# A list scheduler that counts weight transfers at 405 GB/s, and a last expert pair without fillers

## The chip, the cores and the metric

The kernel runs on one NeuronCore of one Trainium2 chip. The metric is the time of one execution on the device in microseconds; the time of the kernel before is the median of three runs. Four compute engines matter here: TensorE (PE, matmuls), VectorE (DVE), ScalarE (ACT) and GpSimd (POOL). SyncE (SP) issues every transfer between memory and the on-chip buffers, and 16 DMA engines carry them out.

## The reference, cut to what matters

A trunk of two layers over 272 tokens (16 meta tokens and 256) of width 1024. Each layer has a mixer and then a mixture of 16 experts; all inputs are float32.

```python
for layer in range(DEPTH):                       # 2
    if layer % 2 == 0:
        h = h + ssd_lru_mixer(rms_norm(h, ...), ...)          # "mixer0"
    else:
        h = h + multiscale_pool_mixer(rms_norm(h, ...), ...)  # "mixer1"
    h = h + hierarchical_moe(rms_norm(h, ffn_norm[layer]), ...)
return rms_norm(h[:, N_META:], norm_final)

def hierarchical_moe(hn, ...):                   # top-1 group, top-2 experts in it
    for e in range(MOE_EXPERTS):                 # 16
        hid = silu(tok @ w_gate[e]) * (tok @ w_up[e])        # 1024 x 512 each
        out = out + gates[:, e:e + 1] * (hid @ w_down[e])    # 512 x 1024
```

The weights of the experts are most of what is moved: 16 experts x 3 matrices x 2 MB in each of two layers, 201 MB of the 234 MB of the whole execution.

## The kernel before, in words

**Tiling.** The tokens of an expert are gathered into 64 slots. The experts are worked off in 8 pairs a layer (`p` = 0 to 7), each expert of a pair on its half of the output partitions. A pair takes 12 weight pieces of 1 MB, each a tile in one of 17 slots of the pool `hs`: 4 gate pieces, 4 up pieces, 4 down pieces. Gate and up pieces hold rows of 512 float32 (2 KB) and down pieces rows of 1024 (4 KB); the down pieces of each layer's last pair are cut by columns instead (256 or 128 float32 in a row), as are all pieces of `w_in` and `w_out` (256).

**What a pair does** (in `moe`): `gate_up` multiplies the gathered tokens by the gate pieces (PSUM tile `gb`, 4 quarters), then by the up pieces (`ub`), and DVE makes the hidden rows `sg`. `combine` adds the output of the pair before to the residual (`cmb`). Behind an odd pair `gather` collects the tokens of the next two pairs (`xgp`). `down` transposes `sg` on PE (`htp`), ACT copies that to `ht`, and PE multiplies by the down pieces (`yb`). `ptrans` (`ppt`, `pgs`) is small work for the next pair. A runtime branch (`overflow`, line 1576) sits behind the sixth pair's products as a barrier.

**What sets the order.** Nothing runs while the source is written: each call is recorded as an `Op` with a duration from `Program.cost`, and `Program.order`, a list scheduler, then fixes each engine's instruction order. It keeps a clock for each engine and one (`pipe`) for the transfers, which follow one another without overlap, each as long as its bytes over 358 GB/s. An operation may start when what it reads has been produced or has landed, by these clocks. Among the operations of an engine that can start within 60 ns of the earliest, the one first in the source goes first. On the chip the order of an engine is fixed; only the waits are real.

**Fillers.** Where the scheduler's clock leaves PE idle, `order` puts transposes of the identity into PE's stream (`wm`, line 735 in the trace), one for each 215, 200, 115, 110 or 100 ns of the gap, by the phase that `mark` has set. They compute nothing that is used. Within the pairs (`moe0p0` to `moe1p7`) there are none, with one exception: the phase `moe1p7`, which is all of the last pair of layer 1.

```python
if e == "PE" and self.filler and (op.phase[-2] != "p" or op.phase == "moe1p7"):
    gap = s - FILL0 - clock[e] if clock[e] else s - 650
    ...
    if op.phase == "moe1p7":
        gap, each = gap + FILL0 - FILL3, 110     # FILL3 = 200
    for _ in range(int(gap / each)):
        out.append(self.filler)
```

The fillers cost nothing on the scheduler's own clock: an operation behind them starts there when it would have started without them.

Of the kernel before, what the change touches and what calls it, by code (L numbers as in the profile page):

```python
# [55 lines left out]
class Program:  # L56
# [67 lines left out]
    def cost(self, key, method, out, reads, k):  # L124
        n = self.cols(out)
        ps_ = any(self.in_psum(r) for r in reads) or self.in_psum(out)
        m = max([n] + [self.cols(r) for r in reads])
        scal = sum(isinstance(k.get(w), bass.AP) for w in ("scale", "bias", "scalar", "scalar1"))
        scal += sum(self.cols(r) == 1 for r in reads if n > 1) if not scal else 0
        if method == "dma_start":  # L130
            dims = [tuple(d) for d in (reads[0] if out.tensor.name in self.bufs else out).ap]
            row = dims[-1][1] if dims[-1][0] == 1 else 1
            total = 1
            for _, q in dims:
                total *= q
            return max(total * 4, total // row * 160) / 358.0
        if key == "PE":
            passes, per = (1, 1 if n >= 256 else 4) if reads[0].dtype == F32R else (2, 2)
            if method == "transpose":
                passes, per = 1, 2  # L140
            share = {64: 2, 32: 4, 16: 4}.get(out.ap[0][1], 1)
            return passes * max(n * per / 2.4 / share, self.cols(reads[0]) / 1.2) + 2
        if key == "A":
            return (51 if ps_ else 94) + m / 1.2 + 93 * (scal + (k.get("accum_out") is not None))
        if method == "memset":
            return 35 + 0.84 * m if key == "G" else 7 + 1.04 * m
        if key == "V":
            if method == "reciprocal":
                return 69 + 6.25 * m
            if method in ("tensor_scalar", "tensor_copy"):  # L150
                return 66 + (1.04 if ps_ else 0.52) * m + 61 * scal
            return 68 + 1.042 * m + 61 * scal
        if method in ("affine_select", "iota"):
            return 170 + 0.57 * m
        return 176 + m * 3.33 if method in ("tensor_scalar", "tensor_copy") else 148 + 2.1 * m
# [225 lines left out]
def kernel(  # L381
# [19 lines left out]
    def ps(name):  # L401
        return prog.tile(psp, [128, 512], F32, "ps", 7, name)

    def one(name, shape, dt=F32):
        return prog.tile(const, shape, dt, name, 1, name)
# [4 lines left out]
    def b2(name):  # L410
        return prog.tile(bp, [128, 512], F32, "b2", 4, name)
# [4 lines left out]
    def mark(name):  # L416
        prog.phase = name
# [13 lines left out]
    def hs_free(n=1):  # L431
        live[0] -= n
# [126 lines left out]
    def pump(reserve=None, most=99):  # L559
        reserve = RES[0] if reserve is None else reserve  # L560
        while wpos[0] < len(wq) and live[0] < NHS - reserve and most > 0:
            most -= 1
            key, fn = wq[wpos[0]]
            pieces[key] = fn()
            wpos[0] += 1
# [871 lines left out]
    def moe(l):  # L1437
# [12 lines left out]
        def build_S(Q):  # L1450
            S = fr(b4("S")[:, : nt * 256]).rearrange("p (i s) -> p i s", i=nt)
            for i in range(nt):
                V.tensor_tensor(S[:, i, :].rearrange("p (e r) -> p e r", e=4),
                                rm[:, i, 4 * Q:4 * Q + 4, None].to_broadcast([128, 4, CAP]),
                                iota64[:, None, :].to_broadcast([128, 4, CAP]), op=ALU.is_equal)
            S_t[Q] = S
# [10 lines left out]
        def gather(Q):  # L1467
            gather_cols(S_t[Q], 256)
# [3 lines left out]
        def gu_quarter(kind, bank, p, q):  # L1472
            c0 = (p % 2) * 128
            ws = pieces[(kind, l, p, q)]
            for k in range(2):
                xk = xgh[q // 2][:, (2 * q + k) % 4, c0:c0 + 128]
                if isinstance(ws[0], list):
                    for c in range(4):
                        for e in range(2):
                            PE.matmul(bank[64 * e:64 * e + 64, c * 128:(c + 1) * 128], xk[:, 64 * e:64 * e + 64],  # L1480
                                      ws[e][k][c], start=False, stop=(k == 1 and c == 3))
                    continue
                for e in range(2):
                    PE.matmul(bank[64 * e:64 * e + 64, :], xk[:, 64 * e:64 * e + 64], ws[e][:, k, :],
                              start=(q == 0 and k == 0), stop=(q == 3 and k == 1))
            if p or q < 3:
                hs_free()
                pump()

        def gate_up(p, gs, gb, ub):  # L1490
            if p:
                for q in range(4):
                    gu_quarter("g", gb, p, q)
            sg = b2("sg")
            A.activation(sg, gb, AF.Silu, scale=gs[:, 1:2])
            if p:
                ub = ps("ub")
                for q in range(4):
                    gu_quarter("u", ub, p, q)
            V.scalar_tensor_tensor(sg, ub, gs[:, 1:2], sg, op0=ALU.mult, op1=ALU.mult)  # L1500
            return sg

        def ptrans(S, g3):

            pp = ps("ppt")
            for i, (o, sz) in enumerate(tl):
                PE.matmul(pp[:, o - off:o - off + sz], S[:, i, :], identr[:, :sz], start=True, stop=True)
            Pt = fr(b1("Pt"))
            A.copy(Pt[:, :NT], pp[:, :NT])
            pg = ps("pgs")  # L1510
            for i, (o, sz) in enumerate(tl):
                PE.matmul(pg[:, 0:3], ff(S[:, i, :]), g3[:, i, :], start=(i == 0), stop=(i == nt - 1))
            gs = prog.tile(bp, [128, 2], F32, "gs", 3, "gs")
            V.tensor_copy(gs[0:64], pg[0:64, 0:3:2])
            V.tensor_copy(gs[64:128], pg[64:128, 1:3])
            return Pt, gs
# [103 lines left out]
        def combine(yh, yl, Pt, c0=0, n=D):  # L1620
            if l == 0:
                for k in range(c0 // 128, (c0 + n) // 128):
                    c = ps("cmb")
                    PE.matmul(c[:, :T], yh[:, k * 128:(k + 1) * 128], Pt, start=True, stop=False)
                    PE.matmul(c[:, :T], yl[:, k * 128:(k + 1) * 128], Pt, start=False, stop=True)
                    V.tensor_tensor(hT[:, k, :], c[:, :T], hT[:, k, :], op=ALU.add)
            else:
                m = min(n, 512)
                for c1 in range(c0, c0 + n, m):
                    for i in range(2):  # L1630
                        c = ps("cmb")[:, 0:m]
                        PE.matmul(c, Pt[:, i * 128:(i + 1) * 128], yh[:, c1:c1 + m], start=True, stop=False)
                        PE.matmul(c, Pt[:, i * 128:(i + 1) * 128], yl[:, c1:c1 + m], start=False, stop=True)
                        V.tensor_tensor(tok[i][:, c1:c1 + m], c, tok[i][:, c1:c1 + m], op=ALU.add)
# [13 lines left out]
        for p in range(8):  # L1648
            mark(f"moe{l}p{p}")
            if (l, p) == (0, 7):  # L1650
                pools()
            if p % 2 == 0 and p < 6:
                build_S(p // 2 + 1)
            if p:
                Pt, gs = ptrans(S_t[p // 2][:, :, (p % 2) * 128:(p % 2) * 128 + 128], gate[:, :, p, :])
                gb = ps("gb")
            sg = gate_up(p, gs, gb, ub)
            if p == 7:
                A.activation(one("sqrt%d" % (l + 1), [128, 1]), sg[:, 0:1], AF.Sqrt, scale=0.0, bias=eps_t)
            if pend:  # L1660
                combine(*pend.pop())
            if p % 2 and p < 7:
                if p == 5:
                    prog.barrier(overflow)
                gather(p // 2 + 1)
                if p == 5:
                    hs_free(2)
                    RES[0] = RES0 if l == 0 else 0
                    pump()
            y = down(p, sg, gs, Pt)  # L1670
            if p < 7:
                pend.append((*y, Pt))
# [166 lines left out]
    slab_end(b1("end"), 16 - len(ends))  # L1839
    assert len(ends) == 16  # L1840
    moe(0)
    dump("h1", hT)
    pump()
# [3 lines left out]
    RES[0] = 0  # L1847
    pump()
    moe(1)
    final()  # L1850
    with tc.manual_schedule():
# [30 lines left out]
```

## Time and profile before

| | us |
|---|---|
| median of 3 runs | 753.37 |
| range of the runs | 751.78 to 756.37 |
| time of the profiled execution | 755.84 |
| span in its trace | 754.2 |
| PE busy | 714.1 |
| DVE, ACT, POOL busy | 313.9, 245.3, 150.4 |

The execution has five stretches: mixer0 to about 240 us, the experts of layer 0 to about 476, mixer1 to about 506, the experts of layer 1 to about 746, and the final norm. Times in the rows below are from the start of the span. Nearly all instructions were recorded through one helper, so they stand under line 102, and the name of the tile written tells them apart.

### The profile page before, as it was taken

Reading aid. Unit: us, or ns where it says so; the run is one execution under the profiler, and the core shown is the slowest. Engines: PE = TensorE matmul, PEld = TensorE weight load, DVE = VectorE, ACT = ScalarE, POOL = GpSimd, SP = SyncE. Lnnn points to the kernel's source line nnn. Section 1 sums busy time; section 2 is a strip of 40 time slices with the busy share of each in tenths; the row PEclk is TensorE's granted clock in tenths of the full one; section 3 lists DMA queues with packets and bytes.
Section 4 is the critical chain, followed back from the end, with each engine's and each line's share of the span. In section 5 each row is a group of like instructions: output and inputs, shape, how many; then the busy total and the mean of one; then the engine's idle time right before and its main releaser. Section 6 shows DMA issues by size and latency. Waiting matters only on the chain. (4 is left out here: it accounts for less than half of the span.)

```text
span 754.2 us, 11128 instructions
## 1 busy us (share of the span) xinstructions
PE 714.1 (95%) x4370; PEld 449.0 (60%) x4370; DVE 313.9 (42%) x701; ACT 245.3 (33%) x466; POOL 150.4 (20%) x149
## 2 busy tenths in 40 slices
PE   7999999997999999999998989989999999989995
PEld 5989889997899536436434433774354433353353
DVE  6779798779955012203221231571021211202204
ACT  4565476774353312113012012543130120121114
POOL 5654675466940000000000030000000000000003
PEclk7999999999999999999999999999999999999998
DMA  8993121937657879999999999988799999999951
GB/s 257 261 349 106 29 91 45 313 113 279 213 201 255 315 297 409 409 409 408 410 409 407 400 403 376 409 351 320 292 409 409 409 408 409 409 407 409 397 155 56
DMA packets 99622, 234.06 MB, mean 310 GB/s; under 512 B 12700, under 2 KB 51800, under 8 KB 99560
## 3 DMA queue, kind: packets, MB, share of 16 engines
q1 hardware_dynamic: 97448, 232.72, 82.2%
q8 instruction: 37, 0.61, 0.3%
q10 hardware_dynamic: 2112, 0.52, 0.3%
q14 instruction: 25, 0.20, 0.1%
HBM read 232.18 MB, written 1.05 MB: 309 GB/s over the span
## 5 line engine op out<-in xcount | busy, mean ns | idle before, releaser
L102 PE MATMUL yb<-w,ht 128*64 128x512 f32 (+2 forms) x592 | 116.4, 544 | 4.5 <-ACT ht L102 4.4
L102 PE MATMUL gb<-w,xg 128*64 128x512 f32 x496 | 115.7, 599 | 0.0
L102 PE MATMUL ub<-w,xg 128*64 128x512 f32 (+1 forms) x514 | 114.3, 583 | 0.1
L102 PE MATMUL pj<-Xh,wh 128*128 128x272 f32 x288 | 86.1, 301 | 1.3 <-DVE xT L102 1.3
L102 PE MATMUL pj<-Xl,wh 128*128 128x272 f32 x288 | 84.9, 295 | 0.0
L102 PE MATMUL pj<-Xh,wl 128*128 128x272 f32 x288 | 84.5, 294 | 0.0
L102 PEld LDWEIGHTS yb<-w,ht 128*64 128x64 f32 x592 | 40.7, 138 | 69.0 <-issue 56.1
L102 DVE SCALAR_TENSOR_TENSOR yl<-yb,gs,yh 128x512 fp32r<-128x512 f32 (+2 forms) x37 | 25.1, 677 | 129.5 <-ACT yh L102 120.3
L102 PEld LDWEIGHTS ub<-w,xg 128*64 128x64 f32 x514 | 36.8, 137 | 67.1 <-issue 65.2
L102 DVE SCALAR_TENSOR_TENSOR sg<-ub,gs,sg 128x512 f32<-128x512 f32 x16 | 12.0, 751 | 147.9 <-PE ub L102 146.6
L102 DVE TENSOR_TENSOR wl<-w,wh 128x1024 fp32r<-128x1024 f32 (+1 forms) x50 | 60.0, 1208 | 16.4 <-PE pj L102 8.8
L102 PEld LDWEIGHTS gb<-w,xg 128*64 128x64 f32 x496 | 32.7, 136 | 56.6 <-issue 49.7
L102 POOL TENSOR_TENSOR fo<-hT,gfin 128x256 f32<-128x256 f32 (+1 forms) x10 | 6.0, 627 | 292.6 <-DVE hT L102 292.4
L102 ACT ACTIVATE xg<-xgp,gain_e 128x256 f32<-128x256 f32 x64 | 30.2, 475 | 88.6 <-PE xgp L102 79.4
L102 POOL TENSOR_SCALAR wh<-w 128x512 fp32r<-128x512 f32 x25 | 52.2, 2087 | 30.6 <-PE pj L102 22.7
L102 PEld LDWEIGHTS pj<-Xh,wh 128*128 128x128 f32 x288 | 55.7, 194 | 2.8 <-DVE xT L102 1.5
L102 DVE TENSOR_TENSOR hT<-cmb,hT 128x272 f32<-128x272 f32 (+3 forms) x102 | 45.1, 495 | 28.1 <-PE cmb L102 28.0
L102 PEld LDWEIGHTS pj<-Xl,wh 128*128 128x128 f32 x288 | 55.8, 194 | 0.2
L102 ACT ACTIVATE yh<-yb,gs 128x512 fp32r<-128x512 f32 (+2 forms) x37 | 23.3, 630 | 99.6 <-PE yb L102 99.6
L102 PEld LDWEIGHTS pj<-Xh,wl 128*128 128x128 f32 x288 | 55.6, 193 | 0.0
L102 ACT CAST wh<-w 128x512 fp32r<-128x512 f32 (+1 forms) x51 | 42.0, 829 | 31.4 <-PE pj L102 18.6
L102 POOL TENSOR_TENSOR wl<-w,wh 128x512 fp32r<-128x512 f32 x29 | 43.5, 1502 | 41.2 <-issue 19.1
(348 smaller groups left out, 1035.4 us busy)
## 6 DMA issues: line engine op xcount, KB each, us to landing
w<-in_expert_w_down_dram SPq DMA_DIRECT2D x63, 1024.0 KB, 16.4
w<-in_expert_w_gate_dram SPq DMA_DIRECT2D x62, 1024.0 KB, 18.1
w<-in_expert_w_up_dram SPq DMA_DIRECT2D x62, 1024.0 KB, 15.3
w<-in_w_in_dram SPq DMA_DIRECT2D x17, 1024.0 KB, 9.6
w<-in_w_out_dram SPq DMA_DIRECT2D x8, 1024.0 KB, 11.4
ew<-in_expert_w_gate_dram SPq DMA_DIRECT2D x4, 512.0 KB
xs<-in_x_dram SPq DMA_DIRECT2D x2, 512.0 KB
w<-in_w_in_dram SPq DMA_DIRECT2D x2, 512.0 KB
```

The source lines that it names most:

```text
L102: return prog.add(key, lambda: call(*a, **k), reads, writes, prog.cost(key, method, out, reads, k), func)
```

## The change

It has two parts. The scheduler's cost of a transfer divides by 405 instead of 358 where the contiguous row has 512 or more elements (2 KB): that holds for the expert pieces other than the last pairs' down pieces, for the input tokens and the final gain, not for `w_in`, `w_out`, the pooling weights or the small parameters. And the phase is called `moe0pg` or `moe1pg` while `gate_up` of the last pair is recorded, so that the condition for fillers does not hold there; afterwards it is `moe0p7` or `moe1p7` again (for the other pairs the second `mark` sets the name that is already set). No operation that computes is added or removed, and no byte more or less is moved.

```diff
@@ Program.cost, method == "dma_start"
-            return max(total * 4, total // row * 160) / 358.0
+            return max(total * 4, total // row * 160) / (405.0 if row >= 512 else 358.0)
@@ moe, loop over the pairs
             if p:
                 Pt, gs = ptrans(S_t[p // 2][:, :, (p % 2) * 128:(p % 2) * 128 + 128], gate[:, :, p, :])
                 gb = ps("gb")
+            if p == 7:
+                mark(f"moe{l}pg")
             sg = gate_up(p, gs, gb, ub)
+            mark(f"moe{l}p{p}")
```

## Rows read from the trace of the kernel before

**Rows 1.** The page, busy time, share of the span and instructions of PE.
```profile
PE 714.1 (95%) x4370; PEld 449.0 (60%) x4370; DVE 313.9 (42%) x701; ACT 245.3 (33%) x466; POOL 150.4 (20%) x149
```

**Rows 2.** What PE waited for from 245 to 745 us: total us, times, longest.
```profile
PE xgp L102 <- PEq L1576: 4.8, 2, 2.5
PE htp L102 <- DVE sg L102: 4.7, 5, 1.0
PE yb L102 <- ACT ht L102: 4.4, 8, 0.7
```

**Rows 3.** Stretches: length, each engine's busy time (instructions), granted clock, DMA share, GB/s.
```profile
280.00:480.00 200.00, 192.60 (x1033) 92.14 (x1030) 50.74 (x133) 37.25 (x71) 6.41 (x28) 0.99 1.03 404
545.00:700.00 155.00, 147.08 (x706) 63.32 (x702) 29.87 (x56) 26.85 (x51) 0.00 (x0) 0.99 1.02 409
```

**Rows 4.** The same view, layer 1, pairs 1 to 7, first down product to first.
```profile
529.85:556.82 26.97, 26.86 (x143) 13.03 (x139) 5.38 (x10) 6.45 (x13) 0.00 (x0) 1.00 0.91 346
556.82:580.88 24.06, 23.90 (x114) 9.53 (x114) 4.87 (x10) 2.91 (x6) 0.00 (x0) 1.00 1.03 409
580.88:613.56 32.68, 30.76 (x147) 13.00 (x147) 5.96 (x14) 6.94 (x14) 0.00 (x0) 1.00 1.02 408
613.56:640.52 26.96, 25.25 (x115) 9.27 (x115) 5.05 (x9) 3.02 (x5) 0.00 (x0) 1.00 1.03 410
640.52:673.30 32.78, 30.19 (x146) 14.39 (x146) 4.86 (x8) 6.50 (x13) 0.00 (x0) 0.95 1.02 407
673.30:700.21 26.91, 25.26 (x114) 9.26 (x115) 5.24 (x11) 3.25 (x6) 0.00 (x0) 1.00 1.02 409
700.21:734.10 33.89, 33.88 (x180) 15.43 (x180) 4.74 (x7) 2.87 (x5) 0.00 (x0) 1.00 0.79 276
```

**Rows 5.** The same view, layer 0, pairs 2 to 5.
```profile
294.70:319.30 24.60, 24.60 (x125) 10.33 (x125) 4.93 (x13) 2.92 (x6) 0.00 (x0) 1.00 1.02 409
319.30:348.73 29.43, 29.43 (x167) 15.13 (x166) 6.59 (x17) 6.76 (x14) 0.00 (x0) 1.00 1.02 409
348.73:375.07 26.34, 25.73 (x127) 10.57 (x128) 5.76 (x15) 3.26 (x6) 0.00 (x0) 1.00 1.03 409
375.07:407.54 32.47, 30.00 (x164) 14.92 (x164) 6.95 (x20) 6.46 (x13) 0.00 (x0) 1.00 1.02 408
```

**Rows 6.** Timeline of PE, pairs 2 and 4 of layer 1: start, length, instructions, [wait].
```profile
570.60 7.04 PE L102 MATMUL ub<-w,xg 128*64 128x512 f32 x32
577.57 0.50 PE L102 MATMUL cmb<-yh,Pt 128*128 128x512 f32 x1
...
579.52 0.63 PE L102 MATMUL htp<-ident,sg 128*128 128x128 f32 x4
...
623.90 0.50 PE L102 MATMUL cmb<-yh,Pt 128*128 128x512 f32 x1
...
639.04 0.74 PE L102 MATMUL htp<-ident,sg 128*128 128x128 f32 x4 [0.92 <-DVE sg L102]
640.52 7.09 PE L102 MATMUL yb<-w,ht 128*64 128x512 f32 x32 [0.73 <-ACT ht L102]
```

**Rows 7.** The chain of work that ended last, in the last pair: start, length, what.
```profile
713.60 1.13 PE wm L735 x9
...
728.60 1.13 PE wm L735 x9
729.74 1.87 PE ub L102 x8
731.60 0.92 PE wm L735 x7
```

**Rows 8.** Timeline of SP: the issues of the last pair's four up pieces.
```profile
686.71 10.60 SPq L102 DMA_DIRECT2D w<-in_expert_w_up_dram  x4
```

**Rows 9.** DMA issues from 686.6 to 686.8 us: KB each, us to landing.
```profile
w<-in_expert_w_up_dram SPq DMA_DIRECT2D x1, 1024.0 KB, 18.9
```

**Rows 10.** Stretches as in rows 3, behind waits of PE.
```profile
401.35:405.00 3.65, 3.65 (x30) 3.65 (x31) 1.48 (x8) 2.23 (x5) 0.00 (x0) 1.00 1.03 406
437.50:440.50 3.00, 3.00 (x8) 0.83 (x10) 0.00 (x0) 0.00 (x0) 0.00 (x0) 0.54 1.03 411
666.60:670.00 3.40, 3.40 (x16) 3.40 (x17) 0.00 (x0) 1.36 (x3) 0.00 (x0) 0.52 1.03 405
```

## The prediction, made before the change was run

> **What bounds the kernel now.** I read the page first: PE is busy for 714.1 of 754.2 us [rows 1]. A busy PE may still be one that others pace, so the waits come next. From 245 to 745 us, both expert layers and mixer1, PE waited 4.8 us for the runtime branch (twice), 4.7 us for `sg`, 4.4 us for `ht`, and for no weight transfer [rows 2]. The transfers look just as full, 404 and 409 GB/s over long stretches [rows 3], so the question is which of the two is ahead. The first up piece of the last pair is issued at 686.71 [rows 8] and lands 18.9 us later [rows 9], at 705.6. The last up quarter starts at 729.74 [rows 7], the first three quarters of 1.87 + 1.13 us before it, at 720.7. So a piece lies ready for 15 us: PE's instruction stream sets the end, and the transfers follow 15 us ahead of it.
>
> The third view is the main one: the same work, pair by pair. Pairs 2 and 4 of layer 1 have 114 and 115 matmul records but take 24.06 and 26.96 us; pairs 1 and 3, which also hold a gather, have 143 and 147 and take 26.97 and 32.68 us [rows 4]. The timeline shows what differs [rows 6]. In pair 2 the combine of the pair before stands behind the last up quarter (577.57), runs while DVE makes `sg`, and `htp` follows without a wait. In pair 4 that combine was spent at 623.90, between two gate quarters, so at the end of the up products PE has nothing left and waits 0.92 us for `sg` and 0.73 us for `ht`. The cutting costs busy time as well, 25.25 against 23.90 us [rows 4]. I call pairs like 2 packed and pairs like 4 broken. All pairs of layer 1 from 3 on are broken; in layer 0 pairs 2 and 3 are packed and pair 4 is broken (26.34 against 24.60 us) [rows 5].
>
> Which it becomes is decided on the scheduler's clock: when it believes that the next piece has not landed, it pulls the combine and the gather into that supposed gap. On the chip no such gap exists.
>
> **The fillers.** Behind six of the last pair's eight quarters stand 9 transposes each, 1.13 us a group, the first at 713.60 and the last at 728.60 [rows 7]. They are on the chain that ended last, and the weights behind them have landed. The change removes all six: 6 x 1.13 = 6.8 us. The seven at 731.60 (0.92 us) stay, because they stand in front of `htp`, whose phase is still `moe1p7`; they cover a wait for `sg` that lasts as long without them. Between the first two gate quarters stands a combine, which stays. Layer 0 had no fillers there, so its new phase name changes nothing.
>
> **The transfer cost.** A piece of 1,048,576 bytes goes from 2.93 to 2.59 us on the scheduler's clock; measured it is 1,048,576 / 409 = 2.56 us [rows 3]. The Trainium skill, "DMA: Bandwidth & Descriptors", section Specifications, gives about 358 GB/s as what memory yields to one core; the trace disagrees, with 409 held for 155 us [rows 3]. By that figure a pair's 12.6 MB would need 35.1 us, longer than every pair in rows 4, and packing would bring nothing.
>
> How far does it carry? By the code's costs a quarter is 4 matmuls x 0.43 = 1.71 us, and a pair of layer 1 is 12 x 1.71 + 0.43 (`htp`) + 0.87 (`ptrans`) + 1.72 (combine) + 1.74 (half a gather) = 25.3 us; layer 0 about 26. (These are the scheduler's beliefs, not times.) Its transfers take 35.1 us a pair, so it falls 9.8 us behind in each pair of layer 1 and 9 in layer 0; at 405 the pair takes 31.1 us and it falls 5.8 and 5 behind. The head start is what it used up before the first broken pair: in layer 0 about 3.5 pairs x 9 = 31 us, which now lasts 6 pairs; in layer 1 about 2.5 x 9.8 = 24 us, which now lasts 4, and more, since the scheduler's transfers no longer drag behind into layer 1. So I expect pairs 4 and 5 of layer 0 and pairs 3 and 4 of layer 1 to be packed, pair 5 probably, pair 6 as an open case.
>
> Each is priced by a packed pair of its kind:
> Layer 1, pair 3: 32.68 - 26.97 = 5.7 us. Pair 4: 26.96 - 24.06 = 2.9. Pair 5: 32.78, less 2.4 for the branch, which stays, less 26.97 = 3.4; a stretch at half clock behind that branch (3.40 us at 0.52 [rows 10]) costs 1.7 of it and may stay, so 1.7 to 3.4. Pair 6: 0 to 2.9 (26.91 - 24.06).
> Layer 0, pair 4: 26.34 - 24.60 = 1.7. Pair 5: 32.47 - 2.4 - 29.43 = 0.6.
>
> mixer0 and mixer1 keep their costs except for the token loads (524,288 bytes, 0.17 us less on the clock) and the expert pieces issued late in mixer0. That can turn near ties of the list scheduler either way. No row prices it; I take 0 and keep 1.7 us, the cost of one half-clock stretch, on both sides.
>
> **The limit.** PE can only gain what it lags. The last up piece lands at 705.6 + 3 x 2.56 = 713.3 and is used at 729.74: 16.4 us. In the last pair's stretch 33.89 us x 276 GB/s = 9.4 MB moved [rows 4]; at 346 to 409 GB/s, the extremes of rows 4 before it, the last down piece landed at 723 to 727, and the last down product stands some 10 us behind the first at 734.10, which gives 17 us: the same limit. The transfers of layer 1 cannot move up against the start of that layer, for they run at 409 GB/s from pair 2 on (346 in the row before it), and slots freed by pairs 0 and 1, packed already, set their start. What layer 0 gains comes on top.
>
> The sum: layer 1 would gain 6.8 + 5.7 + 2.9 + (1.7 to 3.4) = 17.1 to 18.8, cut to 16.4; layer 0 gains 2.3. Together 18.7 us. The span goes from 754.2 to 735.5; the profiled execution's own time, 755.84, to 737.1. That execution lies 2.5 us above the median of the runs, 753.37, from which the same sum gives 734.7. I say 735.5. In the last pair PE then waits for transfers with nothing to fill the wait; behind it on PE stand `htp` and the down products, and for those wait ACT (`ht`, `yh`), DVE and in the end SP's four stores, so each late piece moves the end by its own lateness.
>
> **The rivals.**
> Fewer pairs are packed, only pair 3 of layer 1 and pair 4 of layer 0 beside the fillers: 6.8 + 5.7 + 1.7 = 14.2 us, 740. For it: my head starts are read off to half a pair. It lies in the forecast's range.
> Only the fillers count: 6.8 us, 746.6 from the median. For it: a combine may be pulled forward because a slot or a PSUM bank is late on the scheduler's clock, not a piece. Against it: the broken pairs come late in each layer, as a head start that runs out would make them, and slots and banks are the same in all pairs.
> Slower: the clock. Granted clock fell to 0.54 and 0.52 (1.2 GHz where 1 is 2.4) at 437.50 and 666.60, behind waits of PE of about 1.7 and 2.4 us, and stayed at 1.00 behind another of 2.4 us at 401.35 [rows 10]. Without fillers the last pair waits up to 2.56 - 1.87 = 0.7 us before each quarter. If TensorE then ran the whole last pair at half clock, 33.89 - 6.8 = 27.1 us would double and the 18.7 us turn into a loss of 8.4, 761.8. It decides from 18.7 us of TensorE work at half clock upward. Against it: the waits seen so far cost 3.4 us at half clock, 1.7 us each, and six of these would still leave a gain of 8.5. The Trainium skill, "TensorE: Matmul & The Clock Gate", section HAM oscillation, tells of a kernel that was throttled again at every tile because TensorE waited for each tile's transfer; the trace agrees for two of the three waits in rows 10, and by that rule this rival is what happens.
>
> **How the numbers follow.** The forecast, packed pairs up to the limit or somewhat short of it: 0.84. Only the fillers or nothing: 0.12. The clock: 0.04. The range reaches down to a further even pair packed in layer 0 (2.9) and the 1.7 us of mixer0, about 730, and up to the fillers with one even pair (6.8 + 2.9), about 745. A change of 1%, about 7.5 us, is what a measurement here can tell from none: the forecast lies beyond it, the fillers alone within it.
>
> **What would show it.** Right: no `wm` between the quarters of the last pair; layer 1's pairs 3 and 4 at about 27 and 24 us, with `cmb` behind the up products and no wait of `htp` for `sg`; waits of PE for up or down pieces appear in the last pair only; the transfers' rate stays at 409 GB/s. Wrong: broken pairs from 3 on as before (then about 747), a granted clock below 1 through the last pair, or waits for weights already in the middle of a layer, which would mean that packing has met the transfers earlier than the lag of 15 us says.

## The result, and the profile after

| | before | after |
|---|---|---|
| median of 4 runs, us | 754.38 | 736.38 |
| range of the runs | 751.78 to 756.37 | 735.97 to 738.08 |
| span of the profiled execution | 754.2 | 735.1 |

The ratio is 0.9765, 95% interval 0.9736 to 0.9794. The forecast was 735.5.

The page of the changed kernel, busy time of each engine. PE has 61 instructions fewer than in [rows 1] (4,309 against 4,370) and is busy 17.3 us less; its share of the span is still 95%.

```profile
PE 696.8 (95%) x4309; PEld 442.7 (60%) x4309; DVE 314.8 (43%) x701; ACT 245.2 (33%) x466; POOL 148.8 (20%) x149
```

The stretches of the changed kernel from first down product to first down product: length, busy time (instructions) of PE, PEld, DVE, ACT and POOL, granted clock, DMA share, GB/s. The first four lines are layer 0's pairs 4 to 7, the other five layer 1's pairs 3 to 7; they answer to [rows 4, 5].

```profile
347.88:372.53 24.65, 24.65 (x126) 10.37 (x125) 4.97 (x13) 2.93 (x6) 0.00 (x0) 1.00 1.03 409
372.53:409.74 37.21, 31.26 (x166) 16.79 (x165) 7.37 (x23) 6.69 (x14) 0.00 (x0) 0.91 1.02 408
409.74:434.88 25.14, 25.14 (x127) 10.43 (x126) 5.18 (x13) 2.89 (x5) 0.00 (x0) 1.00 1.03 401
434.88:463.94 29.06, 27.23 (x134) 11.12 (x133) 8.75 (x22) 3.07 (x6) 6.43 (x28) 1.00 1.05 384
...
578.29:606.22 27.93, 27.76 (x146) 13.38 (x147) 5.67 (x13) 6.73 (x14) 0.00 (x0) 1.00 1.02 408
606.22:630.30 24.08, 23.92 (x114) 9.54 (x115) 4.83 (x10) 2.92 (x6) 0.00 (x0) 1.00 1.03 409
630.30:661.76 31.46, 28.82 (x146) 12.84 (x146) 5.18 (x11) 6.71 (x14) 0.00 (x0) 1.00 1.03 408
661.76:688.69 26.93, 25.33 (x114) 9.17 (x114) 5.43 (x11) 3.24 (x6) 0.00 (x0) 1.00 1.02 408
688.69:714.92 26.23, 26.07 (x122) 9.67 (x123) 4.83 (x7) 2.86 (x5) 0.00 (x0) 1.00 1.04 397
```

Read it as three things. Pairs 3 and 4 of layer 1 are packed now (27.93 and 24.08), pairs 5 and 6 aren't, and the last pair is 7.7 us shorter. In layer 0, pairs 4 and 6 are packed. And one pair became longer: pair 5 of layer 0, 37.21 us, with a mean clock of 0.91.

The whole table, pair lengths in us (layer 0's and layer 1's pairs 1 to 7; the experiments are told below). Lengths are differences of the times at which each pair's first down product starts in the timeline of PE.

| kernel | layer 0, pairs 1 to 7 | layer 1, pairs 1 to 7 | sum of layer 1 | span | median |
|---|---|---|---|---|---|
| before | 28.07 24.62 29.42 26.34 32.47 29.88 29.13 | 26.97 24.06 32.68 26.96 32.78 26.91 33.89 | 204.25 | 754.2 | 754.38 |
| after | 28.08 24.62 29.41 24.65 37.21 25.14 29.06 | 26.97 24.06 27.93 24.08 31.46 26.93 26.23 | 187.66 | 735.1 | 736.38 |
| e1_fillers_only | 28.07 24.62 29.42 26.34 32.49 29.88 27.43 | 26.97 24.07 32.68 26.96 32.80 26.89 26.21 | 196.58 | 744.4 | 746.32 |
| e2_rate_only | 28.07 24.62 29.41 24.65 37.55 25.14 29.07 | 26.96 24.07 27.93 24.08 31.33 26.93 31.15 | 192.45 | 741.0 | 742.35 |
| e3_rate_layer1 | 28.07 24.62 29.42 26.34 32.61 29.88 27.43 | 26.96 24.07 27.93 24.08 31.30 26.93 26.22 | 187.49 | 734.4 | 737.92 |
| e4_rate_1000 | 28.07 24.62 29.41 24.65 37.26 24.80 26.26 | 26.96 24.07 27.93 24.08 30.25 24.09 30.72 | 188.10 | 730.9 | 732.32 |
| e5_combine_first | 28.07 24.62 29.42 24.65 33.88 24.80 28.83 | 26.96 24.07 27.93 24.08 31.38 26.94 26.04 | 187.40 | 730.5 | 732.42 |
| e6_both | 28.07 24.62 29.42 24.65 33.96 24.80 28.10 | 26.96 24.07 27.93 24.08 32.32 24.03 28.94 | 188.33 | 729.9 | 730.56 |
| e7_less_gain | 28.07 24.62 29.41 24.65 33.97 24.80 26.73 | 26.96 24.07 27.93 24.08 31.39 24.03 30.64 | 189.10 | 728.1 | 729.19 |
| e8_rate_380 | 28.07 24.62 29.42 24.65 34.55 30.36 27.43 | 26.96 24.07 29.32 27.01 31.24 26.63 26.07 | 191.30 | 741.6 | 743.25 |

From before to after the span falls by 19.1 us: 16.6 in layer 1, 1.7 in layer 0 with mixer1, and 0.85 ahead of layer 0's first down product (265.77 us against 266.62). That start lies between 265.1 and 267.8 us in all ten kernels. With mixer0 in the order of before it was 266.14 in another run (e1), and in the order of after 266.57 (e2), so those 0.85 us are scatter.

The chain of work that ended last, changed kernel, last pair: start, length, what. The six groups of `wm` of [rows 7] are gone and the four up quarters stand in one block; the two groups around `htp` stay.

```profile
679.34 7.04 PE ub L102 x32
...
695.81 1.20 SPq L102
...
697.10 17.69 DMA w<-in_expert_w_down_dram
714.79 0.14 issue
714.92 1.95 PE yb L102 x16
```

The chain leaves PE here. Pair 6's down products end at 695.8 and free a slot, SP issues a down piece of the last pair into it, the piece lands 17.7 us later, and the first down product starts 0.14 us behind that. PE's own work ahead of that product, the group of `wm` behind `htp`, ends at 714.78, so the piece and PE meet within 0.01 us: at this place the 15 us by which the transfers led PE are used up.

### The profile page after: what moved, and what is told of

Same layout as the page of the kernel before. It is cut to its first block, busy times and chain, and to the rows that moved or that the text cites. A ratio compares the mean times of both kernels' runs of the same rounds, so it can differ in the third digit from the quotient of the medians.

```text
span 735.1 us, 10978 instructions
## 1 busy us (share of the span) xinstructions
PE 696.8 (95%) x4309; PEld 442.7 (60%) x4309; DVE 314.8 (43%) x701; ACT 245.2 (33%) x466; POOL 148.8 (20%) x149
## 5 line engine op out<-in xcount | busy, mean ns | idle before, releaser
L102 PE MATMUL yb<-w,ht 128*64 128x512 f32 (+2 forms) x592 | 114.9, 538 | 2.3 <-ACT ht L102 2.0
L102 PE MATMUL gb<-w,xg 128*64 128x512 f32 x496 | 114.0, 597 | 0.0
L102 ACT CAST wh<-w 128x512 fp32r<-128x512 f32 (+1 forms) x51 | 42.0, 829 | 31.8 <-PE pj L102 18.8
L102 POOL TENSOR_TENSOR wl<-w,wh 128x512 fp32r<-128x512 f32 x29 | 41.8, 1445 | 40.6 <-issue 19.1
```

The costliest lines, as they stand in the source:

```text
L102: return prog.add(key, lambda: call(*a, **k), reads, writes, prog.cost(key, method, out, reads, k), func)
```

## The experiments

All diffs are against the kernel after, unless another is named. The medians of e1 to e4 stand against 753.82 us for the kernel before in the same runs, those of e5 to e8 against 754.07.

### e1: the last pair without fillers, the old rate

```diff
-            return max(total * 4, total // row * 160) / (405.0 if row >= 512 else 358.0)
+            return max(total * 4, total // row * 160) / 358.0
```

> The second half of the change alone: transfers stay at 358 GB/s on the scheduler's clock, no fillers among the last pair's gate and up products. My theory: the order of the layers is that of the kernel before, pairs 3 to 6 of layer 1 stay broken (about 32.7, 27.0, 32.8, 26.9 us from first down product to first down product), the last pair loses six groups of 1.13 us and the time falls by 6.8 us, to about 747 (ratio 0.991). PE lags the transfers by 16 us there, so nothing of it is lost. Rival, that the fillers kept TensorE's clock up: a granted clock near 0.5 in the last pair and less gain than 6.8 us, or a loss.

Measured: 746.32 us, ratio 0.9903 (0.9864 to 0.9941). Stretches of this kernel (columns as above), layer 1's pair 3 and last pair:

```profile
578.75:611.43 32.68, 30.77 (x147) 12.99 (x147) 5.95 (x14) 6.91 (x14) 0.00 (x0) 1.00 1.02 408
698.08:724.29 26.21, 26.20 (x125) 10.19 (x126) 4.74 (x7) 2.86 (x5) 0.00 (x0) 1.00 1.00 347
```

Pair 3 is as in [rows 4], to the hundredth. The last pair falls from 33.89 to 26.21, by 7.68 us and not by 6.8: a quarter that stood alone took 1.87 us [rows 7], and four in one block take 7.04 in the kernel after, 1.76 each; seven of the eight quarters (the first gate quarter stays alone) make some 0.8 us of that. The clock stays at 1.00 with no filler in it. Of the rest of the span's gain, 1.7 us is layer 0's pair 7 (29.13 to 27.43): the stretch at half clock at 437.50 us [rows 10] did not come in this execution.

### e2: the new rate, the fillers left in

```diff
-            if p == 7:
-                mark(f"moe{l}pg")
             sg = gate_up(p, gs, gb, ub)
-            mark(f"moe{l}p{p}")
```

> The first half alone: 405 GB/s for rows of 2 KB or more, fillers stay in the last pair. My theory: the pairs of both layers are as in the changed kernel, and the last pair keeps fillers, as many as the scheduler's smaller gap allows: at most (2589 - 1715 - 200) / 110 = 6 behind each of up to six quarters, 36 x 0.125 = 4.5 us; since the last pair of the changed kernel is no later than its transfers by more than 0.2 us, all of that is lost again: about 740 to 741. Rival, that the last pair is bound by its transfers with room to spare: the fillers lie inside the waits and the time is that of the changed kernel, 736.

Measured: 742.35 us, ratio 0.9843 (0.9807 to 0.9879). The last pair of this kernel, and its chain of work there:

```profile
689.70:720.85 31.15, 31.14 (x155) 12.89 (x155) 4.83 (x7) 2.68 (x5) 0.00 (x0) 1.00 1.05 387
```
```profile
705.17 0.80 PE wm L735 x6
...
715.87 0.81 PE wm L735 x6
```

With a cheaper transfer the scheduler sees smaller gaps and puts 6 transposes into each of five gaps instead of 9 (0.81 us instead of 1.13). The stretch has 155 instructions against 122 in the kernel after, and takes 4.9 us longer. That the fillers would sink into waits for transfers (736 us) is refuted: they cost what they last. The time lies 1.4 us above the expected 740 to 741; in the profiled executions 0.8 us of that is the scattering start (266.57 against 265.77) and 0.3 layer 0's pair 5. By the medians the rate alone brings 11.5 us and the end of the fillers alone (e1) 7.5; together they were measured at 18.0. Behind the new rate the fillers are worth 6.0 by the medians (742.35 to 736.38) and 4.9 in the pair itself, since there were fewer of them to take out.

### e3: the new rate for layer 1's expert weights alone

```diff
+            late = "expert_w" in reads[0].tensor.name and reads[0].offset >= NE * D * DE
-            return max(total * 4, total // row * 160) / (405.0 if row >= 512 else 358.0)
+            return max(total * 4, total // row * 160) / (405.0 if row >= 512 and late else 358.0)
```

> 405 GB/s for the expert pieces of layer 1 alone; tokens, layer 0 and the gain stay at 358; no fillers in the last pair. My theory: mixer0 and layer 0 run as before (0.9 and 1.7 us of the gain are missing), layer 1 packs pairs 3 and 4, perhaps one fewer since the head start with which the scheduler enters it is smaller; its gain of 16.6 us from the first down product of pair 0 to that of pair 7 stays within 3 us: 737 to 741. Rival, that the head start is built in layer 0 and carried over: layer 1 breaks at pair 3 as before, only the fillers are saved, 747.

Measured: 737.92 us, ratio 0.98 (0.9755 to 0.9844), span 734.4. Stretches of this kernel: layer 0's pair 5, layer 1's pairs 3, 4 and the last.

```profile
373.59:406.20 32.61, 30.01 (x163) 14.93 (x164) 6.96 (x20) 6.45 (x13) 0.00 (x0) 1.00 1.02 407
577.86:605.79 27.93, 27.77 (x147) 13.38 (x147) 5.68 (x13) 6.73 (x14) 0.00 (x0) 1.00 1.03 409
605.79:629.87 24.08, 23.92 (x115) 9.54 (x115) 4.83 (x10) 2.92 (x6) 0.00 (x0) 1.00 1.02 408
688.10:714.32 26.22, 26.21 (x124) 9.96 (x125) 4.83 (x7) 2.87 (x5) 0.00 (x0) 1.00 1.04 397
```

Layer 1 is that of the kernel after, pair by pair, though layer 0 is that of before. So layer 1's gain needs nothing from layer 0, and layer 0's change gives next to nothing: from its first pair's first down product to the last pair's it takes 198.37 us here, 198.25 in e1 and 198.17 in the kernel after. The 199.93 of before hold 1.7 us of the half clock that e1 did not have. The whole times say less: the four runs of e3 spread from 736.05 to 741.68, its median lies 1.5 us above the kernel after, and the profiled execution is its fastest. The lengths of the pairs carry this reading, not the medians.

### e4: a rate that the memory does not have

```diff
-            return max(total * 4, total // row * 160) / (405.0 if row >= 512 else 358.0)
+            return max(total * 4, total // row * 160) / (1000.0 if row >= 512 else 358.0)
```

> The scheduler counts rows of 2 KB or more with 1000 GB/s, so that on its clock no expert piece is ever late; no fillers in the last pair. My theory: all pairs are packed, pair 6 of layer 1 too (24 us instead of 26.9), but layer 1 cannot end before its last down pieces have landed: PE now waits for pieces of the last pair, and the time is that of the changed kernel within 2 us (735 to 738). Rival, that PE alone is the bound: pairs 6 and 7 of layer 1 and pairs 5 to 7 of layer 0 give another 4 us or more, 732 or less.

Measured: 732.32 us, ratio 0.9706 (0.9672 to 0.974). It lies between the expected 735 to 738 and the 732 or less of the rival that PE alone is the bound, so the time by itself decides for neither; the stretches do. On this clock no transfer is late, so every pair that can be packed is. Stretches of this kernel: layer 1's pair 6, its last pair, and 22 us inside the last; below them PE's waits from 600 to 731 us (total, times, longest).

```profile
656.46:680.55 24.09, 23.98 (x114) 9.44 (x114) 4.78 (x10) 2.91 (x6) 0.00 (x0) 1.00 1.02 408
680.55:711.27 30.72, 25.73 (x115) 8.82 (x115) 4.88 (x10) 4.45 (x7) 0.00 (x0) 1.00 1.04 398
684.00:706.00 22.00, 17.20 (x74) 4.56 (x70) 1.50 (x2) 3.35 (x4) 0.00 (x0) 1.00 1.02 407
```
```profile
PE ub L102 <- DMA w<-in_expert_w_up_dram: 2.5, 4, 0.7
PE gb L102 <- DMA w<-in_expert_w_gate_dram: 2.4, 4, 0.6
```

In layer 1, pairs 5 and 6 gain 4.05 us against the kernel after and the last pair gives back 4.49: PE waits 0.52 to 0.71 us before each of its eight quarters. The sum of layer 1 is 188.1 against 187.7. This is the transfer limit of the prediction, met in the open: with 2.8 to 4.1 us more of packing to be had, the layer does not get shorter. The 4 us by which this kernel is faster come from layer 0, pairs 6 and 7 (24.80 and 26.26 against 25.14 and 29.06, 3.1 us), from mixer1 (0.5), and from the start (0.5) and the tail (0.6). The expected time was missed because it counted nothing for these.

It also tries the rival of the clock, for the kernel after has no waits before quarters: through eight such waits the granted clock is 1.00. The Trainium skill, "TensorE: Matmul & The Clock Gate", section HAM oscillation, tells of a kernel throttled again at every tile that waits for its transfer. The waits that it tells of are several times as long. The last pair of no run here has one of that length, and these of 0.52 to 0.71 us, ahead of 1.94 us of products, did not do it.

### e5: layer 0's pair 5 with its combine ahead of the gate products

```diff
+            if (l, p) == (0, 5):
+                combine(*pend.pop())
             if p == 7:
                 mark(f"moe{l}pg")
             sg = gate_up(p, gs, gb, ub)
```

> The changed kernel, and in the sixth pair of layer 0 the combine of the pair before is recorded ahead of the gate and up products, so that 512-column up products and not short combine matmuls are the last that PE gets before the runtime branch. My theory of layer 0: the branch holds PE's sequencer for 6.0 us in every kernel; what hides part of it is the work already handed to PE, 3.2 us of up products before, 0.3 us of combine in the changed kernel. So PE's wait at the branch goes from 5.95 back to about 2.5 us, the half clock behind it (6.8 us) shrinks or goes, and the time falls by 3.5 to 5.4 us, to 731 to 733. Rival, that the longer wait is another engine's lateness: the wait and the time stay, 736.

Measured: 732.42 us, ratio 0.9716 (0.9689 to 0.9743); against the kernel after 4.0 us less.

In the kernel after, PE before and behind the branch of layer 0 (timeline: start, length, instruction, [wait]), and DVE's first addition of that combine; on PE's sequencer the load of the branch's register and the branch itself (ns, least, median, most; first and last start); and the stretch behind the wait:

```profile
394.60 0.43 DVE L102 TENSOR_TENSOR hT<-cmb,hT 128x272 f32<-128x272 f32 x1
...
395.75 0.29 PE L102 MATMUL cmb<-Pt,yl 128*128 128x272 f32 x1
401.98 0.55 PE L102 MATMUL xgp<-S,hn 128*128 128x256 f32 x1 [5.95 <-PEq L1576]
```
```profile
L1575 PEldq TENSOR_LOAD <-mxi x2: 315/400/486, 395.1 to 649.6; - x2
L1576 PEldq COMPARE_BRANCH  x2: 5988/6050/6112, 395.7 to 650.0; - x2
```
```profile
398.70:405.50 6.80, 3.52 (x16) 3.55 (x17) 1.66 (x8) 0.95 (x2) 0.00 (x0) 0.50 1.03 408
```

The same in e5: timeline of PE, and pair 5 as a stretch.

```profile
393.59 2.31 PE L102 MATMUL ub<-w,xg 128*64 128x512 f32 x10
398.50 0.55 PE L102 MATMUL xgp<-S,hn 128*128 128x256 f32 x1 [2.59 <-PEq L1576]
```
```profile
372.18:406.06 33.88, 31.29 (x166) 16.60 (x166) 7.37 (x23) 6.68 (x14) 0.00 (x0) 0.95 1.02 408
```

The branch holds PE's sequencer for 6.0 to 6.1 us wherever it stands. What differs is how much work PE still had from before it. In e5 it begins at 392.1 us; the up products, handed over before, run on under it until 395.9, and 2.6 us are left to wait. In the kernel after, the combine of the pair before stands there, 16 products of 0.13 us each, and when the branch begins all but the last of them have started; that one is done 0.3 us later: 5.95 us of wait, and 6.8 us at half clock that begin within it.

Why so little was left is not settled by a run, and it is not only that these products are short. In e4, e6 and e7 the same combine stands just ahead of layer 1's branch, as 8 products of 512 columns behind up products, and PE waits there 2.13, 2.69 and 2.84 us. In e4 (timeline of PE):

```profile
648.69 0.39 PE L102 MATMUL cmb<-yl,Pt 128*128 128x512 f32 x1
651.21 0.47 PE L102 MATMUL xgp<-S,hnt 128*128 128x256 f32 x2 [2.13 <-PEq L1576]
```

There 16 products start after the branch has begun; in all 17 short waits of the ten kernels it is 12 to 17, in the three long ones (after, e2, e4) it is 1. In those three, and in no other, the load of the branch's register stands directly behind the end of DVE's first `hT<-cmb` addition: 395.09 against 395.04 us in the kernel after, and 0.05 us apart in e2 and e4 too. That suggests that the sequencer was held until DVE had emptied a PSUM tile for the last products of layer 0's combine, which fills 8 such tiles where layer 1's fills 4; no run moved that alone. So e5 refutes a wait that stays wherever the combine stands, but not DVE's part in it.

The wait makes up pair 5: 32.47, less 0.6 for the packing, 3.5 more of wait, and half of the 3.52 us that PE worked at half clock is 37.1 against 37.21 measured. e2 and e4, whose combine stands there too, show the same 6.8 us and pairs of 37.55 and 37.26. In e5 the half clock lasts 3.4 us and the pair 33.88.

### e6: e4 and e5 together

```diff
-            return max(total * 4, total // row * 160) / (405.0 if row >= 512 else 358.0)
+            return max(total * 4, total // row * 160) / (1000.0 if row >= 512 else 358.0)
...
+            if (l, p) == (0, 5):
+                combine(*pend.pop())
```

> The scheduler's 1000 GB/s together with the combine recorded first in the sixth pair of layer 0. My theory: the two gains lie in different pairs of layer 0 and add up, 732.3 less 3.5 to 5.4 us, 727 to 729; layer 1 keeps its 188 us from the first down product of pair 0 to that of pair 7, set by its transfers. Rival, that what layer 0 gains is lost again to the transfers of layer 1: 731 or more.

Measured: 730.56 us, ratio 0.9691 (0.9657 to 0.9725): the fastest kernel here that moves every byte, 1.8 us below e4 and 1.9 below e5, where the two gains of 4 us each were to add up. It misses the expected 727 to 729 and lies just short of the rival's 731. PE's waits in this kernel from 434 to 731 us:

```profile
PE ub L102 <- DMA w<-in_expert_w_up_dram: 3.8, 6, 0.7
...
PE gb L102 <- DMA w<-in_expert_w_gate_dram: 1.1, 2, 0.6
```

Two of the six waits for up pieces lie in layer 0's pair 7 (0.64 and 0.71 us), where no earlier kernel waited for weights, and the pair takes 28.10 us against 26.26 in e4: now layer 0 meets its transfers too. In e7, which has the same order on PE, one such wait of 0.25 us stands there and the pair takes 26.73. A stretch at half clock in layer 1's pair 5 (32.32 us against 30.25 in e4, which has none there) cost next to nothing in the end: the last pair is 1.8 us shorter than in e4 (28.94 against 30.72), with six waits before its quarters instead of eight, and the sum of layer 1 is 188.33 against 188.10. Where the transfers set the end, what PE loses before it comes out of its waits.

### e7: fewer bytes ahead of the last pieces

Against e6:

```diff
-        SP.dma_start(out=t, in_=norm_final.partition_broadcast(128))
+        SP.dma_start(out=t[:, 0:256], in_=norm_final[0:256].partition_broadcast(128))
...
-                G.tensor_tensor(o[i][:, sl], ms["tok"][i][:, sl], gb[:, sl], op=ALU.mult)
+                G.tensor_tensor(o[i][:, sl], ms["tok"][i][:, sl], gb[:, 0:n], op=ALU.mult)
```

> As the kernel with both, but the final norm's gain, which is loaded ahead of the last pair's down pieces, is loaded for its first 256 columns alone and these are used for all (so 0.39 MB of 234 are left out, and the result is not the reference's). If the transfers of layer 1 set its end, the last down pieces land 0.39 MB / 409 GB/s = 1.0 us earlier and the end comes 0.7 to 1.0 us earlier. Rival, that PE sets it: no difference in the place of the last down products against the first of layer 1.

Measured: 729.19 us, ratio 0.9665 (0.9641 to 0.969), 1.4 us below e6. It leaves out three quarters of the gain, so what it computes is not the reference's. Timeline of PE at the end, first e6, then e7:

```profile
705.15 1.94 PE L102 MATMUL ub<-w,xg 128*64 128x512 f32 x8 [0.63 <-DMA w<-in_expert_w_up_dram]
...
715.46 1.95 PE L102 MATMUL yb<-w,ht 128*64 128x256 f32 x16 [0.30 <-DMA w<-in_expert_w_down_dram]
...
719.71 1.09 PE L102 MATMUL yb<-w,ht 128*64 128x128 f32 x16
```
```profile
704.28 1.94 PE L102 MATMUL ub<-w,xg 128*64 128x512 f32 x8 [0.64 <-DMA w<-in_expert_w_up_dram]
...
713.71 1.95 PE L102 MATMUL yb<-w,ht 128*64 128x256 f32 x16
...
717.95 1.09 PE L102 MATMUL yb<-w,ht 128*64 128x128 f32 x16
```

From the last up quarter to the last down product it is 14.56 us in e6 and 13.67 in e7: 0.9 us less for 0.39 MB, which at 409 GB/s are 0.96 us. The two waits of 0.30 us before down products are gone. So at the end of e6 the bytes set the time, almost one for one. By the measure named beforehand, the last down product against the first of layer 1, the two differ by 0.13 us only (197.75 and 197.62), as the rival has it. That measure misleads here: layer 1's first down product comes 1.63 us earlier in e7, its last up quarter only 0.87 earlier, since both kernels wait there for transfers. The place of 14.56 and 13.67 was chosen after the run, so this is a reading of the traces and not a forecast that came true.

### e8: a rate between the two

```diff
-            return max(total * 4, total // row * 160) / (405.0 if row >= 512 else 358.0)
+            return max(total * 4, total // row * 160) / (380.0 if row >= 512 else 358.0)
```

> The changed kernel with 380 GB/s in place of 405. My theory: by the scheduler's arithmetic a pair of layer 1 then takes 33.1 us of transfers and it falls 7.8 us behind in each, so the head start that lasted 2.5 pairs at 9.8 lasts about 3: pair 3 of layer 1 is packed (28 us), pair 4 broken (26.9), pairs 5 and 6 broken; in layer 0 pair 4 is packed (24.6). Rival, that the orders of the pairs depend on near ties and not on the head start: no such step between 358 and 405.

Measured: 743.25 us, one time. Stretches of this kernel: layer 0's pairs 4 and 6, layer 1's pairs 3 and 4.

```profile
349.93:374.58 24.65, 24.65 (x126) 10.37 (x126) 4.97 (x13) 2.93 (x6) 0.00 (x0) 1.00 1.02 409
409.13:439.49 30.36, 28.71 (x144) 12.22 (x143) 5.85 (x15) 3.27 (x6) 0.00 (x0) 1.00 1.03 403
581.25:610.57 29.32, 29.16 (x146) 13.04 (x146) 5.86 (x13) 6.71 (x14) 0.00 (x0) 1.00 1.03 409
610.57:637.58 27.01, 25.30 (x114) 9.18 (x115) 5.24 (x11) 3.24 (x6) 0.00 (x0) 1.00 1.02 409
```

Layer 0's pair 4 is packed and its pair 6 broken again; layer 1's pair 3 is nearly packed, with no idle left but some cuts, and pair 4 is broken. The boundary between packed and broken pairs moves with the rate on the scheduler's clock, pair by pair, as a head start that runs out makes it. That speaks against slots or PSUM banks that are late on that clock, since the number of neither changes with the rate; it is an argument, no run varied them.

## Why the prediction was right, and where it was not

The mechanism holds in layer 1 and at the fillers, and the total is 0.9 us off by the medians (736.38 against 735.5), 0.4 by the spans (735.1). Its terms are not all as good as that, and in part the total is luck.

**Fillers: 6.8 forecast, 7.7 measured** (e1). Left out was what a quarter saves when it stands in a block again, about 0.1 us for each of seven, beside the 1.13 us of each group.

**Layer 1, pairs 3 and 4: 5.7 and 2.9 forecast, 4.75 and 2.88 measured.** Pair 4 got the price of pair 2, which does the same work with the same number of records. Pair 3 got the price of pair 1, which has 143 records where pair 3 has 147 [rows 4]; a part of pair 1's gate products lies ahead of its stretch. 27.93 is what a packed odd pair costs, not 26.97.

**Layer 1, pair 5: 1.7 to 3.4 forecast, 1.3 measured, and not for the reason given.** Its gate quarters still stand apart, so it is not packed. What it gained is the half-clock stretch of [rows 10] at 666.60 us, which did not come here (the clock is 1.00 throughout). e1, with the order of before and that stretch, has 32.80; e8, not packed there either and without the stretch, has 31.24. Pair 6, the open case, stayed broken: 26.93.

**The limit: 16.4 forecast, 16.6 measured.** The uncut sum of 17.1 to 18.8 was too high; what the schedule offered was 16.6 by itself (7.7 + 4.75 + 2.88 + 1.3), and of that 1.3 hangs on a half-clock stretch that did not come. That the two figures agree is chance: the cut did not act, the terms were smaller. That the limit is real, and lies at that place, the kernel after alone does not show (one wait of 0.14 us). e4 does: more packing, the same length of layer 1. In after, e3, e4, e5 and e6, whose pairs differ by up to 4.7 us, the seven pairs sum up to 187.4 to 188.3 us.

**Layer 0: 2.3 forecast, 1.7 measured, and this is the step that failed.** Pair 4 did as forecast (1.69). Pair 5 was priced as 32.47 - 2.4 - 29.43, with the 2.4 us of the branch as a constant, the one of which layer 1's price says that it "stays". It does not stay in layer 0. Packing moves the combine behind the up products, which is the place just ahead of the branch, and there next to nothing is left to run under it: the wait grew from 2.5 to 5.95 us, half clock followed, and the pair became 4.74 us longer instead of 0.6 shorter.

Pair 6, counted as nothing, was packed and 4.74 us shorter. The two cancel. Pair 7 looks unchanged (29.13 and 29.06), but before had 1.7 us of half clock in it and after has none: against the 27.43 of e1 and e3 it is 1.6 us longer, with 134 instructions on PE instead of 117, work that packing moved there from pair 6. That takes back what pair 4 gave.

By e3 and e1, layer 0's part of the change gives nothing beyond the scatter of half-clock stretches: 198.17 us with it, 198.25 to 198.37 without. The sum came out by luck, through errors that cancel; e5 shows that 4 us lay there.

**mixer0 and mixer1: 0 forecast;** mixer1 63.32 us against 63.30, mixer0 within its scatter.

**The rivals.** Fewer pairs (740): refuted, layer 1's pairs 3 and 4 and layer 0's 4 and 6 are packed. Only the fillers (746.6): e1 is that kernel, 746.32. The clock (761.8): the last pair without fillers ran at 1.00 in after and e1, and at 1.00 through waits of 0.52 to 0.71 us in e4. "Waits of PE for up or down pieces in the last pair" was put down as a sign of the forecast; it came only as 0.14 us before one down product, because layer 1's own gain ended just where the limit begins.

**The transfer rate.** The transfers stayed at 407 to 410 GB/s in the stretches of pairs 2 to 6 of all ten kernels, but for layer 0's pair 6 with 401 to 403. The Trainium skill, "Perfetto Trace Analysis", section Roofline, says that a core which has the memory to itself can go beyond 358 GB/s, up to what its 16 DMA engines carry, some 435; the trace agrees, at 409. By that section the figure that the prediction weighed from another page is a share, not a ceiling for one core.

**Still open:** when a wait of some 2 us brings half clock. Of the 17 waits of 2.1 to 2.8 us for the branch in the ten kernels, 7 have a stretch of 3.4 us at half clock behind them and 10 none, and in layer 0's pair 7 before and e1 differ in that with the same order of instructions. Some 1.5 us of any single forecast hang on it.

## What to carry to other kernels

A list scheduler's belief about transfer time is worth a measurement of its own: a rate 12% too low made PE fetch other work into gaps that did not exist, and cost 11 us of 754. Once it is right, look at what the better order has moved ahead of a fixed cost such as a branch, for that cost is hidden only by work that was handed over before it begins, and price such a cost by its length on the sequencer and not by the wait that is left of it. And when a gain in the middle of a layer comes back as a wait at its end, the transfers have been met, and fewer bytes are what helped here (e7).

## What the runs showed of the hardware

A runtime branch holds PE's sequencer for 6.0 to 6.1 us, in every kernel and both layers; PE's wait for it was 2.1 to 2.8 us where 12 to 17 products started after it had begun (17 cases), and 5.95 to 6.08 where one did (3 cases).

The three waits of 5.95 to 6.08 us (after, e2, e4) each brought 6.8 us at half clock (0.50, the lower level, 1.2 GHz), where the 17 of 2.1 to 2.8 us brought 3.4 or none. Eight waits of 0.52 to 0.71 us, one every 2.6 us, left the clock at 1.00.
